# Two ordinary pairs instead of three at the head of each FFN, with the copies of turned tokens moved and the token sums reordered

## The chip, the cores and the metric

The kernel runs on one core of a Trainium2 chip. The metric is device time of one execution in microseconds (us); lower is better. Engines are named as in the profile: PE (TensorE matmul), PEld (its weight load), DVE (VectorE), ACT (ScalarE), POOL (GpSimd) and SP (SyncE, which here only issues DMAs).

## The reference

One encoder layer on 512 tokens of 1024 features, in float32: a half-step SwiGLU FFN, token mixing by two attention branches, and a second half-step SwiGLU FFN, each between two RMS norms. The change touches the two FFNs:

```python
D_MODEL, SEQ, D_FF = 1024, 512, 2816
def _rmsnorm(x, g):
    y = x * lax.rsqrt(jnp.mean(x * x, axis=-1, keepdims=True) + 1e-6)
    return y * g
def _swiglu(x, w_gate, w_up, w_down):
    return (jax.nn.silu(x @ w_gate) * (x @ w_up)) @ w_down
...
f = _swiglu(_rmsnorm(x, ffn1_pre_g[l]), ffn1_w_gate[l], ffn1_w_up[l], ffn1_w_down[l])
x = x + 0.5 * _rmsnorm(f, ffn1_post_g[l])
h = _rmsnorm(x, mix_pre_g[l])
# ... two attention branches on h, gated, projected, normed and added to x
f = _swiglu(_rmsnorm(x, ffn2_pre_g[l]), ffn2_w_gate[l], ffn2_w_up[l], ffn2_w_down[l])
x = x + 0.5 * _rmsnorm(f, ffn2_post_g[l])
```

## The kernel before

**Exactness.** Each float32 operand is split into a high part (`hi`, a cast to a shorter format, on ACT) and a low part (`lo`, what is left, a subtraction on DVE); `split` does both. A product is then three matmuls (`mm3`): high by high, high by low, low by high (lines 153 to 155).

**Tokens.** After a norm, the tokens are turned (tokens along the free axis) by PE transposes into a PSUM bank `pt`, four feature blocks at a time (`turned`, for token tile `t` of 128 and feature half `b`). From `pt`, ACT writes `hn_hi` and DVE `hn_lo`. For the last 256 tokens (`t > 1`), ACT also keeps the unsplit value in four tiles `whole[b][i]`, as long as the list `whole` is not empty.

**A pair.** `gate` and `up` of 128 hidden features make a pair `j`; an FFN has 22 (`NF`). An ordinary pair takes two pieces of weights (128x1024 each) and does 2 x 8 x 3 = 48 matmuls of 512 columns. The first two pairs are done together in `first_pairs`: four projections over tokens 0 to 255, with the turning of tokens 256 to 511 put between them, then the same four over tokens 256 to 511. `use` makes the hidden value of a pair: SiLU on ACT and a multiplication on DVE (line 436).

**Seven products.** The remaining pairs go through `seven`, a scheme of Strassen's kind over (gate, up) x (two feature halves) x (two token halves): seven products of 4 x 3 matmuls of 256 columns instead of eight, 84 in all for a pair. Its moving operands 1, 2 and 4 are plain parts of `hn`; 3, 5, 6 and 7 are sums over tokens, made and split once for each FFN by `combined` (lines 242 and 235 on DVE, 85 and 86 for the split into tiles `v`). Its stationary operands are blocks of weights and their sums: `load_blocks` loads five (four DMAs on SP's queue, and two DMAs that accumulate, on POOL's queue, lines 266 and 267), `sums_of` makes two more on DVE (lines 272, 273), and `split_block` splits each into a tile `w`. `ready(j, i)` does this for block `i` of pair `j`, one pair ahead of the products.

**Order.** The program is written in one order, and a planner lays out the queue of each engine from it with its own estimate of times: what is ready and was written earlier goes first. An engine then works through its queue in that fixed order. In some stretches (`ordered`) the written order is kept as it is on PE, ACT and DVE: from the start of the kernel, or from the last part of `token_major`, up to the end of the matmuls of `first_pairs`. `use`, `combined` and `seven` lie outside. On SP the written order is kept up to the end of the first FFN. Tiles come from pools: 54 `unit` tiles of 128x512, 12 tiles `w`, 2 tiles `raw`, and 8 PSUM banks; a tile is given back after its last use in the program.

**Streams.** `fetch` converts the next piece of weights of the ordinary stream, up to `state["stop"]`, and calls `state["ahead"]` where there is none. At the end of each FFN the products of the down projection follow in `token_major`. The mixing between the FFNs calls `first_pairs` too, with `then` making copies of all turned tokens in another order (`v_proj_na`; line 524 on ACT, 526 on DVE).

Of the kernel before, what the change touches and what calls it, by code (L numbers as in the profile page):

```python
# [12 lines left out]
F32 = mybir.dt.float32  # L13
# [18 lines left out]
SPREAD = 4  # L32
URGENT = 400
TURN = 1
STD = 3
WARM = (0, 0, 0, 5, 15)
PINNED = (mybir.EngineType.PE, mybir.EngineType.Activation, mybir.EngineType.DVE)

# [2 lines left out]
def block_kernel(ctx, tc, x, gains, weights, rpb_near, rpb_all, alibi0, alibi12, out):  # L41
# [13 lines left out]
    def unit(dt=F32, name="u"):  # L55
        return up.tile([P, 512], dt, tag="u", name=name)
# [27 lines left out]
    def split(hi, lo, src):  # L84
        nc.scalar.copy(hi, src)  # L85
        nc.vector.tensor_tensor(lo, src, hi.bitcast(F32), op=ALU.subtract)  # L86
# [56 lines left out]
    late = deque()  # L143
    next_norm = []
    whole = []

    def step(n=1):
        for _ in range(n):
# [22 lines left out]
    def first_pairs(use, turns, then=None):  # L171

        w = [take(False) for _ in range(4)]
        ps = [bank() for _ in range(4)]
        for i in range(4):
            proj_into(ps[i], w[i], 0, 256)
            if i in turns:
                late.popleft()()
                if next_norm:
                    next_norm.pop()()  # L180
        if then:
            then()
        fetch()
        fetch()
        for i in range(4):
            proj_into(ps[i], w[i], 256, 512)
        ordered[-1].append(mark())
        use(0, *ps[:2])
        use(1, *ps[2:])
# [28 lines left out]
    def turned(t, b, xs):  # L218
        pt = bank()
        for i in range(4):  # L220
            nc.tensor.transpose(pt[:, i * P:(i + 1) * P], xs[:, i * P:(i + 1) * P], ident)  # L221
        to = (slice(None), slice(4 * b, 4 * b + 4), slice(t * P, (t + 1) * P))
        pt = pt.rearrange("p (k t) -> p k t", t=P)
        nc.scalar.copy(hn_hi[to], pt)
        nc.vector.tensor_tensor(hn_lo[to], pt, hn_hi[to].bitcast(F32), op=ALU.subtract)
        if whole and t > 1:
            for i in range(2):
                o = whole[b][i].rearrange("p (k t) -> p k t", k=2)
                nc.scalar.copy(o[:, :, (t - 2) * P:(t - 1) * P], pt[:, 2 * i:2 * i + 2])

    def combined():


        sub, add = ALU.subtract, ALU.add
        tt = lambda a, b, op: (lambda u: [nc.vector.tensor_tensor(u, a, b, op=op), u][1])(unit(name="sum"))
        view = lambda a, b, i: a[:, 4 * b + 2 * i:4 * b + 2 * i + 2, 0:256]
        flat = lambda u: u.rearrange("p (k t) -> p k t", k=2)
        mv = {i: [] for i in (3, 5, 6, 7)}
        for i in range(2):
            a = [unit(name="sum"), unit(name="sum")]  # L240
            for b in range(2):
                nc.vector.tensor_tensor(flat(a[b]), view(hn_hi, b, i).bitcast(F32), view(hn_lo, b, i).bitcast(F32), op=add)
            c, d = whole[0][i], whole[1][i]
            v = {7: tt(a[0], c, sub), 5: tt(c, d, sub)}
            v[6] = tt(v[5], a[0], sub)
            v[3] = tt(v[6], a[1], add)
            for n in (5, 6, 3, 7):
                hi, lo = unit(F32R, "v"), unit(F32R, "v")
                split(hi, lo, v[n])
                mv[n] += [(hi[:, k * 256:k * 256 + 256], lo[:, k * 256:k * 256 + 256]) for k in range(2)]  # L250
        whole.clear()
        for n, b, t in ((1, 0, 0), (2, 1, 0), (4, 1, 1)):
            mv[n] = [(hn_hi[:, 4 * b + k, t * 256:t * 256 + 256], hn_lo[:, 4 * b + k, t * 256:t * 256 + 256])
                     for k in range(4)]
        return mv

    def load_blocks(n):


        r = wp.tile([P, PIECE], F32, tag="raw", name="raw", bufs=2)  # L260
        w11, t1, t3 = unit(name="w11"), unit(name="t1"), unit(name="t3")
        nc.sync.dma_start(t1, weights[n + 1][:, :512])
        nc.sync.dma_start(t3, weights[n + 1][:, :512])
        nc.sync.dma_start(r, weights[n])
        nc.sync.dma_start(w11, weights[n + 1][:, 512:])
        nc.gpsimd.dma_start(t1, weights[n][:, :512], accum_op=ALU.add)
        nc.gpsimd.dma_start(t3, weights[n + 1][:, 512:], accum_op=ALU.add)
        return {1: r[:, :512], 2: r[:, 512:], 3: w11, 5: t1, 7: t3}
# [9 lines left out]
        split(w[:, :512], w[:, 512:], raw)  # L278
        return w

    def seven(use, mv, n_pairs, n0, behind):

        raws = {}
        blocks = {}
        o = {}

        def get(j):
            if j < n_pairs:
                raws[j] = load_blocks(n0 + 2 * j)

        def ready(j, i):
            if j < n_pairs:
                if j and loads:
                    loads.popleft()()
                if i == 1:
                    sums_of(raws[j])  # L300
                blocks[j, i] = split_block(raws[j].pop(i))
            elif behind:
                behind()

        def product(j, i, key, start):
            if start:
                o[key, j] = bank(key)
            w = blocks.pop((j, i))
            acc = o[key, j][:, :256]
            for k in range(4):  # L310
                mm3(acc, w[:, k * P:(k + 1) * P], w[:, 512 + k * P:512 + (k + 1) * P], *mv[i][k],
                    start and k == 0, k == 3, skip_group_check=True)
            return acc

        res = {}
        get(0)
        get(1)
        for i in (1, 5, 2, 6, 3, 7, 4):
            ready(0, i)
        for j in range(n_pairs + 1):  # L320
            now, was = j < n_pairs, j > 0
            get(j + 2)
            if now:
                q = product(j, 1, "q", True)
                g, u = res[j] = unit(name="g"), unit(name="up")
                nc.scalar.copy(g[:, :256], q)
            ready(j + 1, 1)
            if was:
                q0 = product(j - 1, 7, "q", False)
                g0, u0 = res.pop(j - 1)  # L330
                nc.vector.tensor_tensor(u0[:, 256:], u0[:, 256:], q0, op=ALU.subtract)
            ready(j + 1, 5)
            if now:
                p = product(j, 5, "p", True)
                nc.scalar.copy(u[:, 256:], p)
            ready(j + 1, 2)
            if now:
                r = product(j, 2, "r", True)
                nc.vector.tensor_tensor(g[:, :256], g[:, :256], r, op=ALU.add)
            ready(j + 1, 6)  # L340
            if now:
                product(j, 6, "q", False)
                nc.scalar.copy(u[:, :256], q)
            ready(j + 1, 3)
            if was:
                product(j - 1, 4, "q", False)
                use(j - 1, g0, u0, q0)
            ready(j + 1, 7)
            if now:
                product(j, 3, "p", False)  # L350
                nc.vector.tensor_tensor(u[:, :256], p, u[:, :256], op=ALU.subtract)
            ready(j + 1, 4)
# [68 lines left out]
    def ffn(g, store, src):  # L421
        hidden = [None] * NF
        parts = {}
        n0 = state["take"]

        def stat(k):
            if k not in parts:
                parts[k] = unit(F32R), unit(F32R)
                split(*parts[k], hidden[k])
                hidden[k] = None  # L430
            return parts[k]

        def use(j, pg, pu):
            h = unit(name="h")
            nc.scalar.activation(h, pg, AF.Silu)
            nc.vector.tensor_tensor(h, pu, h, op=ALU.mult)
            hidden[j] = h

        def use7(j, g, u, q):
            nc.scalar.activation(g[:, :256], g[:, :256], AF.Silu)  # L440
            nc.scalar.activation(g[:, 256:], q, AF.Silu)
            nc.vector.tensor_tensor(g, u, g, op=ALU.mult)
            hidden[STD + j] = g

        first_pairs(use, (0, 2) if store else (1, 2))
        mv = combined()
        g_post, g_pre = gain(g), None if store else gain(g + 1)
        for j in range(2, STD):
            pair(use, j)
        if not store:  # L450
            bias_plan()
        after = n0 + 2 * NF
        state["stop"] = total if store else total - 3 * NF + 2 * STD

        def behind():
            state["next"] = max(state["next"], after)
            state["take"] = after
            fetch()

        seven(use7, mv, NF - STD, n0 + 2 * STD, behind)  # L460
        token_major(NF, stat, g_post, 4.0, g_pre, store, src)


# [647 lines left out]
```

## Time and profile before

| | |
|---|---|
| time, median of 3 runs | 1131.28 us (1131.22 to 1131.42) |
| the profiled execution | 1130.41 us |
| its span, first to last instruction | 1128.6 us |
| mean granted TensorE clock | 0.996 |
| PE busy | 1113.6 us (99%) |
| DVE busy | 720.1 us (64%) |
| ACT busy | 582.6 us (52%) |
| POOL busy | 99.7 us (9%) |
| DMA, mean over the span | 138 GB/s |

A row of the timeline gives start, duration, engine, line, operation, what is written and read, shapes and the count of like instructions in a row; in brackets stands how long the engine was idle before, and what ended that. Matmuls are pipelined: a row of 0.28 us may be followed by the next start after 0.12 us, so PE's rate is read from starts. A row of the waits gives total us, how often, and the longest. A row of the windows gives a stretch, then for each engine its busy us and its count of instructions, the granted clock, the share of the DMA engines and GB/s.

### The profile page before, as it was taken

The page shows a single profiled execution, that of the slowest core. Times are in us where ns is not written, and L with a number is a line of the kernel's source. Part 1 is how long each engine was busy: PE and PEld are TensorE (multiplying, and loading weights), DVE is VectorE, ACT ScalarE, POOL GpSimd, SP SyncE. Part 2 cuts the span into 40 slices and gives each one's busy share as a digit, 9 for nine tenths or more (in the row PEclk, how much of TensorE's full clock was granted, in tenths as well). Part 3 has the DMA queues.
Part 4 walks back from the last instruction along what each step waited for, and adds up shares of the span by engine and source line. Part 5 has one row for each costly group of instructions (what it writes and reads, how often), then busy time and mean ns, then how long its engine had stood idle before and what let it go on. Part 6 is the DMA issues. An engine that isn't in the chain of part 4 may idle for free.

```text
span 1128.6 us, 18242 instructions
## 1 busy us (share of the span) xinstructions
PE 1113.6 (99%) x6956; PEld 1005.7 (89%) x6956; DVE 720.1 (64%) x1327; ACT 582.6 (52%) x1188; POOL 99.7 (9%) x157
## 2 busy tenths in 40 slices
PE   8999999999999999999999999999999999999997
PEld 6899999998888988888988888889899999998886
DVE  5797777773245677877486635655787777782312
ACT  5465555572233676767646632345555555571210
POOL 3111221000002000000000000013111111100001
PEclk8999999999999999999999999999999999999999
DMA  6789988443353353322223223353687677443511
GB/s 217 193 191 242 247 222 194 118 126 113 99 156 124 103 169 115 124 89 76 76 81 90 79 79 100 89 181 109 154 215 173 169 192 187 122 132 97 170 51 74
DMA packets 77430, 156.23 MB, mean 138 GB/s; under 512 B 22048, under 2 KB 24096, under 8 KB 77344
## 3 DMA queue, kind: packets, MB, share of 16 engines
q1 hardware_dynamic: 64000, 134.96, 37.7%
q0 software_dynamic: 10944, 19.93, 11.2%
q8 instruction: 54, 0.88, 0.3%
q10 hardware_dynamic: 2400, 0.20, 0.1%
q14 instruction: 32, 0.26, 0.1%
HBM read 150.02 MB, written 7.58 MB: 140 GB/s over the span
## 4 chain that ended last, share of the span: by engine, by line
PE 94%; DVE 2%; ACT 1%; DMA 1%; issue 0%; SPq 0%; DVEq 0%; POOLq 0%; POOL 0%; ACTq 0%
PE ps L153 18%; PE ps L154 18%; PE ps L155 18%; PE q L155 6%; PE q L154 6%; PE q L153 6%; PE p L155 3%; PE p L153 3%; PE p L154 3%; PE r L155 2%; PE r L153 2%; PE r L154 2%; PE ps L661 1%; PE ps L221 1%; PE ps L688 1%; PE ps L630 1%
## 5 line engine op out<-in xcount | busy, mean ns | idle before, releaser
L86 DVE TENSOR_TENSOR w<-raw,w 128x1024 fp32r<-128x1024 f32 (+1 forms) x200 | 195.0, 979 | 217.7 <-ACT w L85 211.4
L85 ACT CAST w<-raw 128x1024 fp32r<-128x1024 f32 (+1 forms) x200 | 169.6, 853 | 239.9 <-PE ps L154 162.8
L153 PE MATMUL ps<-hn_hi,w 128*128 128x512 f32 (+1 forms) x512 | 181.3, 355 | 0.0
L154 PE MATMUL ps<-hn_lo,w 128*128 128x512 f32 (+1 forms) x512 | 179.5, 351 | 0.0
L155 PE MATMUL ps<-hn_hi,w 128*128 128x512 f32 (+1 forms) x512 | 179.2, 350 | 0.0
L153 PE MATMUL ps<-w,u 128*128 128x512 f32 (+1 forms) x456 | 177.3, 389 | 0.0
L154 PE MATMUL ps<-w,u 128*128 128x512 f32 (+1 forms) x456 | 176.9, 388 | 0.0
L155 PE MATMUL ps<-w,u 128*128 128x512 f32 (+1 forms) x456 | 176.8, 388 | 0.0
L86 DVE TENSOR_TENSOR w<-t,w 128x512 fp32r<-128x512 f32 x152 | 104.3, 689 | 28.1 <-ACT w L85 28.1
L85 ACT CAST w<-t 128x512 fp32r<-128x512 f32 x152 | 93.7, 619 | 43.1 <-DVE t L272 18.4
L155 PEld LDWEIGHTS ps<-hn_hi,w 128*128 128x128 f32 x512 | 97.0, 189 | 12.8
L154 PEld LDWEIGHTS ps<-hn_lo,w 128*128 128x128 f32 x512 | 97.2, 190 | 11.6
L153 PEld LDWEIGHTS ps<-hn_hi,w 128*128 128x128 f32 x512 | 97.1, 190 | 11.8 <-issue 0.3
L155 PEld LDWEIGHTS ps<-w,u 128*128 128x128 f32 x456 | 85.7, 188 | 17.5
L154 PEld LDWEIGHTS ps<-w,u 128*128 128x128 f32 x456 | 85.7, 188 | 17.0
L153 PEld LDWEIGHTS ps<-w,u 128*128 128x128 f32 x456 | 85.7, 188 | 16.9
L155 PE MATMUL q<-hn_hi,w 128*128 128x256 f32 x304 | 86.4, 284 | 1.8 <-DVE w L86 1.8
L155 PE MATMUL p<-v,w 128*128 128x256 f32 x304 | 85.9, 284 | 0.9 <-DVE w L86 0.9
L154 PE MATMUL q<-v,w 128*128 128x256 f32 x304 | 86.2, 283 | 0.0
L153 PE MATMUL p<-v,w 128*128 128x256 f32 x304 | 86.2, 283 | 0.0
L155 PE MATMUL q<-v,w 128*128 128x256 f32 x304 | 86.2, 283 | 0.0
L154 PE MATMUL q<-hn_lo,w 128*128 128x256 f32 x304 | 86.2, 283 | 0.0
(149 smaller groups left out, 2299.8 us busy)
## 6 DMA issues: line engine op xcount, KB each, us to landing
raw<-in_weights_dram SPq DMA_DIRECT2D x156, 512.0 KB
t<-in_weights_dram SPq DMA_DIRECT2D x76, 256.0 KB
t<-in_weights_dram POOLq DMA_DIRECT2D x76, 256.0 KB, 5.5
w<-in_weights_dram SPq DMA_DIRECT2D x38, 256.0 KB
x<-in_x_dram SPq DMA_DIRECT2D x16, 256.0 KB
gain<-in_gains_dram SPq DMA_DIRECT2D x6, 512.0 KB
table<-bias_d SPq DMA_DIRECT2D x12, 256.0 KB
table<-in_alibi_dram SPq DMA_DIRECT2D x8, 256.0 KB
```

The source lines that it names most:

```text
L85: nc.scalar.copy(hi, src)
L86: nc.vector.tensor_tensor(lo, src, hi.bitcast(F32), op=ALU.subtract)
L153: nc.tensor.matmul(o, sh, mh, start=start, stop=False, **kw)
L154: nc.tensor.matmul(o, sh, ml, start=False, stop=False, **kw)
L155: nc.tensor.matmul(o, sl, mh, start=False, stop=stop, **kw)
L221: nc.tensor.transpose(pt[:, i * P:(i + 1) * P], xs[:, i * P:(i + 1) * P], ident)
L630: nc.tensor.matmul(ps[:, o:o + w], q[:, cols], windows(wide, kl, i), start=False, stop=True)
L661: nc.tensor.transpose(ps[:, i * P:(i + 1) * P], s, ident)
L688: nc.tensor.matmul(o, vv[n][:, h], m, start=first, stop=(n == 3 and part == 1), skip_group_check=True)
```

## The change

`STD`, the number of ordinary pairs, goes from 3 to 2, so each FFN has 20 pairs in `seven` where it had 19. The copies into `whole` are no longer issued in `turned`; they are collected in `kept` and issued by `first_pairs` after its first four half projections. `load_blocks` for the first two pairs of `seven` is called from the two `fetch` calls in `first_pairs`, by way of `state["ahead"]`. `combined` becomes a generator: first four sums of `hn_hi` and `hn_lo`, then, at each `next`, the sums and splits of operand 5, 6, 3 and 7 in turn, called from the loop that readies the first blocks, whose order becomes 1, 2, 5, 6, 3, 7, 4. `whole.clear()` now stands behind the last `yield`.

```diff
-STD = 3
+STD = 2
...
+    kept = deque()
...
     def first_pairs(use, turns, then=None):
...
+        while kept:
+            kept.popleft()()
         if then:
             then()
         fetch()
...
         if whole and t > 1:
-            for i in range(2):
-                o = whole[b][i].rearrange("p (k t) -> p k t", k=2)
-                nc.scalar.copy(o[:, :, (t - 2) * P:(t - 1) * P], pt[:, 2 * i:2 * i + 2])
+            kept.append(lambda: keep(t, b, pt))
+
+    def keep(t, b, pt):
+        for i in range(2):
+            o = whole[b][i].rearrange("p (k t) -> p k t", k=2)
+            nc.scalar.copy(o[:, :, (t - 2) * P:(t - 1) * P], pt[:, 2 * i:2 * i + 2])
...
     def combined():
...
-        whole.clear()
+        mv = {}
         for n, b, t in ((1, 0, 0), (2, 1, 0), (4, 1, 1)):
             mv[n] = [(hn_hi[:, 4 * b + k, t * 256:t * 256 + 256], hn_lo[:, 4 * b + k, t * 256:t * 256 + 256])
                      for k in range(4)]
-        return mv
+        a = [[unit(name="sum"), unit(name="sum")] for _ in range(2)]
+        for b in range(2):
+            for i in range(2):
+                nc.vector.tensor_tensor(flat(a[b][i]), view(hn_hi, b, i).bitcast(F32), view(hn_lo, b, i).bitcast(F32), op=add)
+        yield mv
+        v = {}
+        for n, of in ((5, lambda i: (whole[0][i], whole[1][i], sub)), (6, lambda i: (v[5][i], a[0][i], sub)),
+                      (3, lambda i: (v[6][i], a[1][i], add)), (7, lambda i: (a[0][i], whole[0][i], sub))):
+            v[n] = [tt(*of(i)) for i in range(2)]
+            mv[n] = []
+            for i in range(2):
+                hi, lo = unit(F32R, "v"), unit(F32R, "v")
+                split(hi, lo, v[n][i])
+                mv[n] += [(hi[:, k * 256:k * 256 + 256], lo[:, k * 256:k * 256 + 256]) for k in range(2)]
+            yield mv
+        whole.clear()
...
-    def seven(use, mv, n_pairs, n0, behind):
+    def seven(use, sums, n_pairs, n0, behind, raws):
...
-            if j < n_pairs:
+            if j < n_pairs and j not in raws:
                 raws[j] = load_blocks(n0 + 2 * j)
...
-        for i in (1, 5, 2, 6, 3, 7, 4):
+        for i in (1, 2, 5, 6, 3, 7, 4):
             ready(0, i)
+            if i not in (1, 2, 4):
+                mv = next(sums)
...
+        raws = {}
+
+        def soon():
+            if len(raws) < 2:
+                raws[len(raws)] = load_blocks(n0 + 2 * STD + 2 * len(raws))
+
+        state["ahead"] = soon
         first_pairs(use, (0, 2) if store else (1, 2))
-        mv = combined()
+        state["ahead"] = lambda: None
+        sums = combined()
+        next(sums)
...
-        seven(use7, mv, NF - STD, n0 + 2 * STD, behind)
+        seven(use7, sums, NF - STD, n0 + 2 * STD, behind, raws)
```

More of the change, by code (lines that the diff above doesn't have):

```diff
@@ L237, in combined @@
         flat = lambda u: u.rearrange("p (k t) -> p k t", k=2)
[L238 to L250, printed above, removed]
-        whole.clear()
+        mv = {}
         for n, b, t in ((1, 0, 0), (2, 1, 0), (4, 1, 1)):
@@ L279, in split_block @@
         return w
-    def seven(use, mv, n_pairs, n0, behind):
-        raws = {}
+    def seven(use, sums, n_pairs, n0, behind, raws):
         blocks = {}
```

## The prediction

> **What bounds the kernel now.** I read the page first, then PE's waits, then PE's pace by windows, and last the timeline of DVE around the two FFN heads.
>
> ```profile
> span 1128.6 us, 18242 instructions
> PE 1113.6 (99%) x6956; PEld 1005.7 (89%) x6956; DVE 720.1 (64%) x1327; ACT 582.6 (52%) x1188; POOL 99.7 (9%) x157
> ...
> PE ps L221 <- DVE u L960: 3.1, 1, 3.1
> PE q L155 <- DVE w L86: 1.8, 2, 1.2
> PE p L155 <- DVE w L86: 0.9, 1, 0.9
> PE ps L629 <- DVE u L86: 0.8, 1, 0.8
> ```
>
> PE is busy from end to end. Of its waits, the first is the start of the kernel; the next two rows, 2.7 us in three places, are the heads of the two FFNs, where products wait for the low parts of weight blocks. A matmul row of 0.28 us outlasts its slot of 0.12, which hides 0.16 us at each place, so the heads cost 2.7 + 3 x 0.16 = 3.2 us. Everything else must come from PE's work itself, or from new waits.
>
> ```profile
> core 0: us, PE busy (x) PEld busy (x) DVE busy (x) ACT busy (x) POOL busy (x), PEclk, DMA share, GB/s
> 40.71:51.62 10.91, 10.91 (x51) 9.02 (x49) 9.91 (x16) 5.43 (x10) 3.52 (x4) 1.00 0.97 238
> 51.62:61.70 10.08, 8.86 (x73) 8.66 (x72) 9.81 (x17) 7.77 (x18) 0.00 (x0) 1.00 0.36 88
> 100.00:110.08 10.08, 10.08 (x86) 10.08 (x85) 8.35 (x16) 6.62 (x16) 1.77 (x2) 1.00 0.99 235
> 808.40:818.10 9.70, 8.17 (x66) 7.77 (x65) 9.70 (x17) 8.76 (x19) 0.67 (x1) 1.00 0.42 135
> ```
>
> The first window is the third ordinary pair of the first FFN: 48 matmuls (three more overlap its edges) in 10.91 us, 0.227 us each. The third is a pair of seven products in full flow: 84 (two more at the edges) in 10.08 us, 0.120 each, without a wait. The second and fourth are the first seven products of each FFN: DVE busy 9.81 of 10.08 and 9.70 of 9.70, PE idle. At a head DVE is the bound.
>
> **The pair exchanged.** Each FFN gives up 10.91 us of PE and takes 10.08: 2 x 0.83 = 1.66 us less. The ACT and DVE work of the twentieth seven-pair, and its larger loads, lie in a stage where DVE is busy 8.35 of 10.08 and PE does not wait: nothing. The pieces no longer converted free ACT and DVE before the head, which is counted below.
>
> **The head without its cover.** How DVE's queue runs at the second FFN's head, and the first's:
>
> ```profile
> 785.33 0.69 DVE L225 TENSOR_TENSOR hn_lo<-ps,hn_hi 128x512 fp32r<-128x512 f32 x1 [1.20 <-ACT hn_hi L224]
> 793.77 0.69 DVE L436 TENSOR_TENSOR h<-ps,h 128x512 f32<-128x512 f32 x1 [7.75 <-PE ps L155]
> 794.38 1.28 DVE L242 TENSOR_TENSOR sum<-hn_hi,hn_lo 128x512 f32<-128x512 f32 x2
> 795.58 0.69 DVE L235 TENSOR_TENSOR sum<-sum,whole 128x512 f32<-128x512 f32 x1
> 796.18 0.69 DVE L235 TENSOR_TENSOR sum<-whole 128x512 f32<-128x512 f32 x1
> 796.90 0.69 DVE L235 TENSOR_TENSOR sum<-sum 128x512 f32<-128x512 f32 x1
> 799.53 0.69 DVE L436 TENSOR_TENSOR h<-ps,h 128x512 f32<-128x512 f32 x1 [1.94 <-PE ps L155]
> 800.14 0.68 DVE L235 TENSOR_TENSOR sum<-sum 128x512 f32<-128x512 f32 x1
> ...
> 33.83 1.23 DVE L86 TENSOR_TENSOR w<-raw,w 128x1024 fp32r<-128x1024 f32 x1 [0.35 <-ACT w L85]
> 35.15 0.69 DVE L436 TENSOR_TENSOR h<-ps,h 128x512 f32<-128x512 f32 x1
> 35.76 1.28 DVE L242 TENSOR_TENSOR sum<-hn_hi,hn_lo 128x512 f32<-128x512 f32 x2
> 40.98 0.69 DVE L436 TENSOR_TENSOR h<-ps,h 128x512 f32<-128x512 f32 x1 [2.01 <-PE ps L155]
> 51.89 0.69 DVE L436 TENSOR_TENSOR h<-ps,h 128x512 f32<-128x512 f32 x1 [0.93 <-PE ps L155]
> ...
> 817.84 0.42 DVE L339 TENSOR_TENSOR g<-g,r 128x256 f32<-128x256 f32 x1
> 818.17 0.69 DVE L86 TENSOR_TENSOR w<-t,w 128x512 fp32r<-128x512 f32 x1
> ```
>
> Three readings. A 128x512 instruction takes 0.60 us from start to start (794.38 to 795.58 for two), a small one 0.33 (817.84 to 818.17). The token sums (L242) read only tokens that were turned long before, yet at both heads none runs before the first pair's multiplication (L436), even with DVE idle 7.75 us. And DVE waits in line: at 799.53 it sat 1.94 us before a multiplication while the sum behind it had its inputs at 797.6.
>
> Now the tally. Before PE can start the second seven-pair, DVE does in the changed head: 2 multiplications, 4 sums L242, 8 sums L235, 8 low parts of `v`, 2 sums of blocks, 7 low parts of blocks, and 3 for the next pair (two sums, one low part): 34 x 0.60 = 20.4, and two small additions, 0.7: 21.1 us. The method holds before: 35 such instructions from 35.06 (with a third multiplication), 21.0 + 0.7, and waits of 2.01 + 0.93 give 59.7; five products from 51.62 on need 5 x 12 x 0.120 = 7.2, to 58.8. It gives 0.9 us of wait where the window shows 1.2.
>
> ```profile
> 782.82 0.59 ACT L224 CAST hn_hi<-ps 128x512 fp32r<-128x512 f32 x1 [1.76 <-PE ps L221]
> 376.28 1.08 ACT L224 CAST hn_hi<-ps 128x512 fp32r<-128x512 f32 x2 [4.58 <-PE ps L221]
> 376.90 1.29 DVE L225 TENSOR_TENSOR hn_lo<-ps,hn_hi 128x512 fp32r<-128x512 f32 x2 [3.04 <-ACT hn_hi L224]
> 25.27 1.03 PE L221 MATMUL ps<-ident,u 128*128 128x128 f32 x8
> ...
> 781.77 0.33 SPq L262 DMA_DIRECT2D t<-in_weights_dram  x1
> 787.14 0.94 POOL L266 DMA_DIRECT2D t<-in_weights_dram  x1 [8.76 <-DMA t<-in_weights_dram]
> ```
>
> Second FFN: with the `whole` copies gone from between, both low parts of the last tokens end 1.9 us after the first cast (376.28 to 378.2), at 782.82 + 1.9 = 784.7, where DVE is free. Block loads start no later than now (781.77) and their accumulation is issued by 788, so the low parts of blocks 1, 2 and 5 (1.8 us) can come early. The first multiplication comes at 791.9: 793.77, less eight of the third pair's matmuls that now stand among the second halves (8 x 0.23 = 1.9). DVE waits 7.2 - 1.8 = 5.4 us. Then that multiplication, the four L242 and one more (five stood there before) take 3.6, to 795.5; the second multiplication cannot start before 799.53 - 1.9 = 797.7: 2.2 more. DVE is done at 784.7 + 21.1 + 5.4 + 2.2 = 813.4. PE ends the second halves at 797.4 and has seven products (1, 2, 5, 6, 3, 7 and 4) for 10.1 us, to 807.5. It waits 5.9 us. First FFN: four of the last eight transposes are done at 25.8 (half of 25.27 to 26.3), and 1.9 later, at 27.7, DVE is free; the multiplications come at 35.0 and 41.0, the second halves end at 40.7. The same sum gives 27.7 + 21.1 + 5.5 + 2.4 = 56.7 against 50.8, 5.9 again. Together 11.8 against 3.2 now: 8.6 us more. From both sides: none of these waits on DVE, and PE waits 0; no early blocks and product 4 only behind the second pair's first, 5.9 + 1.8 + 1.4 = 9.1 a head. I take 5.9, from how both heads ran.
>
> **Copies.** In the FFNs eight copies (2.6 us of ACT) move behind the casts; their readers, the sums for operand 5, come after 791.9, so this costs nothing unless the sums start early. But `whole` is no longer emptied: the generator is left at its last `yield`. So the mixing between the FFNs now makes eight copies it did not make:
>
> ```profile
> 30.63 0.65 ACT L229 COPY whole<-ps 128x256 f32<-128x256 f32 x2 [0.76 <-DVE hn_lo L225]
> 377.24 9.16 ACT L524 CAST u<-hn_hi 128x128 fp32r<-128x128 f32 x16
> 386.31 1.04 ACT L85 CAST w<-raw 128x1024 fp32r<-128x1024 f32 x1
> 387.38 1.23 DVE L86 TENSOR_TENSOR w<-raw,w 128x1024 fp32r<-128x1024 f32 x1 [4.23 <-ACT w L85]
> 391.35 0.40 PE L155 MATMUL ps<-w,u 128*128 128x512 f32 x1
> 398.50 0.36 PE L629 MATMUL ps<-u 128*128 128x256 f32 x1 [0.80 <-DVE u L86]
> ```
>
> Four times 0.65 is 2.6 us, in front of the 16 copies that `then` makes. The weights' low part, which PE needs at 391.35, is done at 388.6: 2.7 us of slack, just used up. The scores at 398.50 already wait 0.80; their chain hangs on the same ACT queue. Between 0 (the planner puts other matmuls ahead) and 2.6 (the whole delay on PE) I take 0.5, nearer to 0 as more such matmuls are at hand. Four units held longer: nothing.
>
> **Loads moved.** Each `soon` issues four DMAs on SP and two on POOL, ahead of the gains' loads on SP. The gains are read hundreds of us later: nothing. In the first FFN POOL's two issues may stand ahead of the norm of the last tokens; I take 0 for it, with an upper bound of 2 us, the two issues at about 1 us each.
>
> **Sum.** -1.7 + 8.6 + 0.5 = +7.4 us. The profiled execution took 1130.41 (span 1128.6 and 1.8 around it), 0.9 under the median of 1131.28; on the median: 1138.7 us.
>
> **The rivals.** *DVE does not wait* (faster): the planner brings the four L242, the sums for operand 5 and the early blocks ahead of the first multiplication. Then 784.7 + 21.1 = 805.8 is before 807.5, and PE waits nowhere: -1.7 - 3.2 + 0.5 = -4.4, 1126.9 us. For it: data and blocks are there sooner than before, and at both heads DVE has time. Against: neither head shows one sum ahead of its multiplication. It decides where DVE's waits at a head, 7.6 us, fall under about 3.9: then PE waits 2.2 a head and the gain pays for it. *Half of it*: one head fills the wait, the other not, or both partly: about 1131, no change that can be told; a measurement of this kernel tells 0.2%, 2.3 us. *The clock falls*: PE's waits come in one piece and the granted clock drops, as after the 3.1 us at the start:
>
> ```profile
> 12.00:16.00 4.00, 4.00 (x16) 2.75 (x15) 3.24 (x5) 3.88 (x8) 2.43 (x2) 0.50 0.88 341
> ```
>
> Four us at 0.50 lose 2 us, for two heads 4: 1142.7. The waits here come between products, at most 2 us each, and the windows with PE idle 1.2 and 1.5 us kept 1.00. The Trainium skill (TensorE: Matmul & The Clock Gate, Part 1: The HAM clock gate) says that the clock halves after an idle window of about 3.4 us; by that rule my waits keep it, and one long wait would not. The trace agrees at its start.
>
> **How the numbers follow.** Slower as worked out 0.57, with the fall of the clock 0.06; half of it 0.17; DVE does not wait 0.20. The likeliest alone is 1133.8 (second waits filled, -4.4, mixing 0) to 1144. The whole range, 1126.5 to 1144, reaches to the faster rival, since the cases have both signs. Faster 0.20, same 0.15, slower 0.65.
>
> **What would show it.** Right: DVE idle before the first and second L436 of each head, L242 behind it, PE's waits on DVE at `p` and `q` several times today's 2.7 us, spread over the first seven-pair; 84 matmuls each 10.08 us after it; eight L229 at 377 us. Wrong: L242 and L235 before the first L436 and no waits of PE.

## The result, and the profile after

The changed kernel takes 1142.37 us (median; 1141.74 to 1146.02), the kernel before 1131.25 beside it: a ratio of 1.0105, 95% interval 1.0084 to 1.0127. It is 11.1 us slower. The profile is of the execution that took 1146.02.

The head of the page:

```profile
span 1144.2 us, 18459 instructions
PE 1118.0 (98%) x7028; PEld 1012.5 (88%) x7028; DVE 730.1 (64%) x1347; ACT 591.7 (52%) x1214; POOL 102.9 (9%) x161
```

PE has 72 matmuls more than the 6956 of before (two seven-pairs of 84 for two ordinary pairs of 48) and 4.4 us more of busy time, and the span is 15.6 us longer: PE waits. Of the 15.6 us, 11.3 lie in the two FFNs (worked out below), 3.05 in the mixing between them and about 1 at the start. Its waits (total us, times, longest):

```profile
PE p L154 <- ACT v L85: 5.5, 2, 2.7
PE q L154 <- ACT g L335: 4.7, 2, 2.4
PE ps L224 <- DVE u L978: 4.7, 1, 4.7
PE ps L679 <- DVE u L667: 1.9, 2, 1.7
```

The first two rows are new: at each head PE waits once for the cast of operand 5 (`v`) and once for ACT's copy of product 1 out of bank `q`, which product 6 is to fill further. Two shorter waits, 0.7 and 0.3 us, follow at the second head. Before, the heads showed only 2.7 us, for low parts of blocks. The last two rows are the start and a place in the mixing; both are longer in this execution (3.1 us before at the start).

The first two seven-pairs of each FFN by windows: before (the first two rows), after (the next two), then a stretch of the first changed head. Behind the busy times stands the granted clock.

```profile
51.62:73.24 21.62, 20.40 (x169) 20.20 (x168) 21.35 (x38) 14.96 (x33) 1.73 (x2) 1.00 0.60 134
808.36:830.55 22.19, 20.66 (x170) 20.26 (x168) 21.23 (x38) 15.66 (x34) 3.94 (x5) 1.00 0.74 204
```

```profile
41.11:69.83 28.72, 23.72 (x170) 23.32 (x169) 27.91 (x48) 17.77 (x37) 3.41 (x4) 0.88 0.63 139
807.16:835.82 28.66, 22.48 (x170) 21.66 (x169) 28.08 (x49) 17.57 (x36) 5.21 (x6) 0.94 0.73 183
46.00:50.00 4.00, 4.00 (x23) 4.00 (x22) 4.00 (x8) 0.07 (x1) 0.00 (x0) 0.57 0.57 147
```

168 matmuls at 0.120 us are 20.16. Before, these stretches lost 1.5 and 2.0 us; now they lose 8.6 and 8.5, with DVE busy nearly throughout. In 46 to 50, PE starts 23 matmuls where 0.120 us would allow 33.

DVE at the first head, then at the second:

```profile
35.62 0.69 DVE L445 TENSOR_TENSOR h<-ps,h 128x512 f32<-128x512 f32 x1 [4.01 <-PE ps L156]
...
36.83 2.49 DVE L251 TENSOR_TENSOR sum<-hn_hi,hn_lo 128x512 f32<-128x512 f32 x4
...
41.38 0.69 DVE L445 TENSOR_TENSOR h<-ps,h 128x512 f32<-128x512 f32 x1 [1.46 <-PE ps L156]
...
42.59 1.29 DVE L241 TENSOR_TENSOR sum<-whole 128x512 f32<-128x512 f32 x2
43.79 0.69 DVE L86 TENSOR_TENSOR w<-t,w 128x512 fp32r<-128x512 f32 x1
...
48.01 1.29 DVE L86 TENSOR_TENSOR v<-sum,v 128x512 fp32r<-128x512 f32 x2
...
799.86 0.69 DVE L86 TENSOR_TENSOR w<-t,w 128x512 fp32r<-128x512 f32 x1 [5.41 <-ACT w L85]
801.60 0.69 DVE L445 TENSOR_TENSOR h<-ps,h 128x512 f32<-128x512 f32 x1 [1.05 <-PE ps L156]
802.21 2.49 DVE L251 TENSOR_TENSOR sum<-hn_hi,hn_lo 128x512 f32<-128x512 f32 x4
...
807.43 0.69 DVE L445 TENSOR_TENSOR h<-ps,h 128x512 f32<-128x512 f32 x1 [2.13 <-PE ps L156]
```

This is the order that was forecast. The token sums (line 242 before, 251 now) run only behind the first multiplication (436 before, 445 now), with DVE idle 4.0 us and 6.5 us (5.41 and 1.05) ahead of it, and the sums for operand 5 only behind the second. The low parts of the blocks then stand ahead of those of operand 5. Then PE, at each wait of the two heads, and ACT's last casts of `v`:

```profile
42.43 0.28 PE L156 MATMUL q<-hn_hi,w 128*128 128x256 f32 x1
45.45 0.39 PE L154 MATMUL p<-v,w 128*128 128x256 f32 x1 [2.75 <-ACT v L85]
...
54.12 0.28 PE L156 MATMUL r<-hn_hi,w 128*128 128x256 f32 x1
56.65 0.58 PE L154 MATMUL q<-v,w 128*128 128x256 f32 x1 [2.25 <-ACT g L335]
57.02 0.42 PE L155 MATMUL q<-v,w 128*128 128x256 f32 x1
57.24 0.41 PE L156 MATMUL q<-v,w 128*128 128x256 f32 x1
...
819.97 0.28 PE L156 MATMUL r<-hn_hi,w 128*128 128x256 f32 x1
822.69 0.38 PE L154 MATMUL q<-v,w 128*128 128x256 f32 x1 [2.45 <-ACT g L335]
822.92 0.28 PE L155 MATMUL q<-v,w 128*128 128x256 f32 x1
```

```profile
55.10 1.22 ACT L85 CAST v<-sum 128x512 fp32r<-128x512 f32 x2 [1.36 <-DVE sum L241]
56.23 0.37 ACT L335 COPY g<-q 128x256 f32<-128x256 f32 x1
```

Less its slot of 0.12 us, the first wait cost 2.90 us at each head, the second 2.41 and 2.60 (a start at 56.65 instead of 54.24). The copy that ended the second stands in ACT's queue behind the casts of all operands, and these wait for DVE's sums. By PE's starts over the 168 matmuls, the longer waits add up to 5.3 and 6.8 us, and slow matmuls (0.213 instead of 0.120 us, 57.02 to 57.24 for one) to 3.1 and 1.7.

The whole of an FFN by PE's starts, from its first projection to its last product: before 236.80 and 236.62 us, after 242.51 and 242.25. The two differences, 5.71 and 5.63, make 11.3: all of the change lies there. The kernel with the kept list emptied (in the table below) has the same heads and 242.49 and 242.25 us in an execution of 1140.84 us, so these stretches are not peculiar to the slower execution that was profiled here.

### The profile page after: what moved, and what is told of

It reads as the page before. It is cut to its first block, busy times and chain, and to the rows that moved or that the text cites. A ratio compares the mean times of both kernels' runs of the same rounds, so it can differ in the third digit from the quotient of the medians.

```text
span 1144.2 us, 18459 instructions
## 1 busy us (share of the span) xinstructions
PE 1118.0 (98%) x7028; PEld 1012.5 (88%) x7028; DVE 730.1 (64%) x1347; ACT 591.7 (52%) x1214; POOL 102.9 (9%) x161
## 4 chain that ended last, share of the span: by engine, by line
PE 92%; DVE 3%; ACT 3%; DMA 1%; issue 1%; SPq 0%; DVEq 0%; POOLq 0%; POOL 0%; ACTq 0%
PE ps L154 18%; PE ps L155 18%; PE ps L156 18%; PE q L154 7%; PE q L156 7%; PE q L155 7%; PE p L154 3%; PE p L155 3%; PE p L156 3%; PE r L155 2%; PE r L154 2%; PE r L156 2%; PE ps L679 1%; PE ps L224 1%; PE ps L706 1%; DVE w L86 1%
## 5 line engine op out<-in xcount | busy, mean ns | idle before, releaser
L154 PE MATMUL ps<-hn_hi,w 128*128 128x512 f32 (+1 forms) x480 | 169.4, 353 | 0.0
L155 PE MATMUL ps<-hn_lo,w 128*128 128x512 f32 (+1 forms) x480 | 167.4, 349 | 0.0
L156 PE MATMUL ps<-hn_hi,w 128*128 128x512 f32 (+1 forms) x480 | 167.1, 348 | 0.0
L86 DVE TENSOR_TENSOR w<-t,w 128x512 fp32r<-128x512 f32 x160 | 109.7, 688 | 34.5 <-ACT w L85 34.0
L85 ACT CAST w<-t 128x512 fp32r<-128x512 f32 x160 | 99.0, 620 | 40.3 <-ACT w L85 18.9
L156 PEld LDWEIGHTS ps<-hn_hi,w 128*128 128x128 f32 x480 | 91.2, 190 | 11.7
L154 PEld LDWEIGHTS ps<-hn_hi,w 128*128 128x128 f32 x480 | 91.3, 190 | 10.6
L155 PEld LDWEIGHTS ps<-hn_lo,w 128*128 128x128 f32 x480 | 91.4, 190 | 10.4
L154 PE MATMUL p<-v,w 128*128 128x256 f32 x320 | 91.3, 286 | 5.8 <-ACT v L85 5.5
L154 PE MATMUL q<-v,w 128*128 128x256 f32 x320 | 91.4, 286 | 4.7 <-ACT g L335 4.7
L154 PE MATMUL q<-hn_hi,w 128*128 128x256 f32 x320 | 90.9, 285 | 0.7 <-ACT w L85 0.7
L155 PE MATMUL q<-v,w 128*128 128x256 f32 x320 | 91.1, 285 | 0.0
L156 PE MATMUL q<-v,w 128*128 128x256 f32 x320 | 91.1, 285 | 0.0
L155 PE MATMUL q<-hn_lo,w 128*128 128x256 f32 x320 | 90.9, 284 | 0.0
```

The lines of the kernel that those rows point to most:

```text
L154: nc.tensor.matmul(o, sh, mh, start=start, stop=False, **kw)
L155: nc.tensor.matmul(o, sh, ml, start=False, stop=False, **kw)
L156: nc.tensor.matmul(o, sl, mh, start=False, stop=stop, **kw)
```

## The experiments

Two numbers say how each kernel's FFNs went: the same stretch in FFN 1 and 2, from its profile, in us. The ratio is to the kernel before as it was measured beside each (medians 1131.10 to 1131.25).

| kernel | us | ratio, 95% interval | FFN 1 | FFN 2 |
|---|---|---|---|---|
| before | 1131.25 | 1 | 236.80 | 236.62 |
| changed | 1142.37 | 1.0105 (1.0084, 1.0127) | 242.51 | 242.25 |
| three pairs, new order | 1139.16 | 1.0072 (1.0057, 1.0087) | 245.12 | 236.97 |
| two pairs, old order | 1150.86 | 1.0181 (1.0164, 1.0198) | 247.43 | 246.31 |
| kept list emptied | 1141.23 | 1.0092 (1.0077, 1.0107) | 242.49 | 242.25 |
| operands 5 and 6 early | 1135.45 | 1.0043 (1.0028, 1.0058) | 239.81 | 238.35 |
| product 2 before 5 | 1142.56 | 1.0097 (1.0084, 1.0111) | 242.48 | 243.08 |
| first wait filled | 1142.67 | 1.0099 (1.0086, 1.0113) | 242.82 | 242.94 |
| all sums early, two pairs | 1128.43 | 0.9977 (0.9968, 0.9986) | 236.29 | 235.98 |
| all sums early, three pairs | 1128.52 | 0.9974 (0.9965, 0.9984) | 236.89 | 234.59 |
| and emptied, two pairs | 1128.90 | 0.9981 (0.9972, 0.9989) | 236.02 | 235.98 |
| and blocks first, two pairs | 1129.10 | 0.9983 (0.9974, 0.9992) | 235.78 | 235.61 |
| and blocks first, three pairs | 1129.30 | 0.9983 (0.9974, 0.9992) | 237.56 | 234.59 |

**The parts of the change alone.** `-STD = 2` `+STD = 3` in the changed kernel:

> The changed kernel with three ordinary pairs again; everything else of the change stays. My theory: the cover over DVE's queue is what was lost. In the two stretches of the first two seven-pairs the changed kernel spent 28.7 us (41.11 to 69.83, and 807.16 to 835.82) on 168 matmuls that take 20.2 at 0.120 us; the kernel before spent 21.6 and 22.2. With 10.9 us of ordinary matmuls between the first pairs and the products again, DVE's queue is ahead and the heads lose 1 to 2 us each as before: 1128 to 1133 us, 9 to 14 under the changed kernel's 1142.4. Rival, the new order of sums and copies itself costs (block casts ahead of operand 5's cast on ACT, the copies in the mixing): the 10.9 us of cover then hide only part and the time stays above 1135.

`-STD = 3` `+STD = 2` in the kernel before:

> The kernel before with two ordinary pairs and nothing else of the change. My theory: the same DVE tally at each head with the same multiplications in front of it, and the sums of all operands in one block; the heads lose at least what they lose in the changed kernel (8.5 us each), so 1142 to 1150 us. If the new order of sums and blocks is what costs, this kernel is clearly faster than the changed one, 1131 to 1138 us.

The first expectation was wrong and its rival held: the time stayed above 1135. The second was right in its theory, and 0.9 us above its range. Two pairs alone cost 19.7 us, and the new order then saves 8.5; with three pairs the new order costs 8.0. The two-pair kernel in the old order puts all operands ahead of the blocks, and PE waits for the first blocks in one piece at each head:

```profile
PE q L153 <- ACT w L85: 9.4, 1, 9.4
PE p L153 <- ACT w L85: 9.2, 1, 9.2
```

With three pairs in the new order, DVE at the first head:

```profile
34.68 2.49 DVE L251 TENSOR_TENSOR sum<-hn_hi,hn_lo 128x512 f32<-128x512 f32 x4
...
46.36 0.69 DVE L86 TENSOR_TENSOR w<-raw,w 128x512 fp32r<-128x512 f32 x1 [5.84 <-ACT w L85]
50.66 0.69 DVE L445 TENSOR_TENSOR h<-ps,h 128x512 f32<-128x512 f32 x1 [3.61 <-PE ps L156]
...
53.68 1.29 DVE L241 TENSOR_TENSOR sum<-whole 128x512 f32<-128x512 f32 x2
```

The stretch from 31 us to the end of its third pair, and the same window of the kernel before:

```profile
31.00:50.50 19.50, 19.50 (x122) 17.61 (x121) 5.03 (x8) 3.34 (x6) 5.45 (x6) 1.00 0.90 222
```

```profile
31.00:50.50 19.50, 19.50 (x127) 17.80 (x126) 15.69 (x24) 8.70 (x16) 5.51 (x6) 1.00 0.84 219
```

DVE worked 5.0 us in this stretch where it had worked 15.7. The generator puts the sums of operands 5, 6, 3 and 7 behind the third pair in the written order, and here they run behind its multiplication at 50.66. So cover alone is not the cause, as I had it: DVE must also have the work ahead of the multiplications. In the second FFN the same kernel lost only 0.35 us against before, and there DVE's queue had another order:

```profile
807.80 1.29 DVE L241 TENSOR_TENSOR sum<-whole 128x512 f32<-128x512 f32 x2
...
817.23 0.68 DVE L445 TENSOR_TENSOR h<-ps,h 128x512 f32<-128x512 f32 x1
```

Between the second multiplication, at 805.87, and the third, at 817.23, stood 12 instructions, among them operand 5's sums and the low parts of blocks; in the first FFN a single one stood there. That agrees with the reading.

**The copies in the mixing.** `+next(sums, None)` behind the loop that readies the first blocks, so that the kept list is emptied:

> The changed kernel with one more step of the generator after the first blocks, so that the list of kept tokens is emptied and the mixing makes no eight copies. The prediction's step: 0.5 us faster (bounds 0 and 2.6). From the traces since: the first scores of the mixing came 6.67 us late in the changed kernel, exactly as late as the first projections of the mixing, so the eight copies (2.3 us on ACT) cost nothing: within 0.5 us of the changed kernel, 1142. If the 3.05 us that the profiled execution lost between the first score and the second FFN come from the copies: 1139 us.

It was 1.1 us faster than the changed kernel, more than the 0.5 expected, but with intervals that overlap (1.0077 to 1.0107 against 1.0084 to 1.0127). With all sums early the emptied list gave 1128.90 against 1128.43, again with intervals that overlap:

> All sums early and two pairs, and besides the list of kept tokens emptied behind the last sum, so that the mixing makes no eight copies. The prediction's step: 0.5 us less than all sums early (bounds 0 and 2.6), so 1127.9. From the traces since, in which the mixing was as long with the copies as without, up to its first scores: 0, 1128.4 us.

In the changed kernel the copies are there, ahead of the 16 of `then`:

```profile
383.90 2.33 ACT L235 COPY whole<-ps 128x256 f32<-128x256 f32 x8
386.02 9.16 ACT L542 CAST u<-hn_hi 128x128 fp32r<-128x128 f32 x16
```

From the first projection of the mixing to its first score PE took 30.21 us before and 30.22 after: the copies cost nothing there. The 3.05 us that the changed kernel's profile lost later in the mixing are absent from the other kernels with the copies (from the mixing's first projection to the second FFN's 409.59 us in the changed kernel, 406.06 with all sums early, 407.37 with the first wait filled, the longest of them, and 406.54 before).

**DVE's order itself.** The sums are drawn from the generator inside `first_pairs`, in the stretch whose written order is kept:

```diff
...
-        first_pairs(use, (0, 2) if store else (1, 2))
+        sums = combined()
+        first_pairs(use, (0, 2) if store else (1, 2), lambda: [next(sums) for _ in range(3)])
         state["ahead"] = lambda: None
-        sums = combined()
-        next(sums)
```

> The changed kernel with the four token sums and the sums and splits of operands 5 and 6 issued inside the first pairs, behind the first four half projections (in the stretch whose written order is kept), so that DVE does them in the 4 to 5 us in which it stood idle ahead of the first multiplication: 12 instructions of 0.60 us, 7.2 us. My theory (DVE in line behind the multiplications is what PE waits for): PE's waits of 5.5 us on operand 5's cast and 4.7 on the copy of product 1 in the profile of the changed kernel go almost wholly, the clock keeps, and 11 to 15 us come back: 1127 to 1132 us. Rival (the order in the queues of PE and ACT: the block casts ahead of operand 5's cast, the copy of product 1 behind the casts of all operands): operand 5's wait goes since its cast is early, but the copy is still behind the casts of 3 and 7 and the blocks, so that about half stays: 1135 to 1138 us.

The 1135.45 us lie in the rival's range, but the profile does not bear the rival out: the wait for the copy was 0.7 us in all. What was left were 3.9 us of waits for low parts of blocks, 1.6 for casts of blocks and some 16 slow matmuls at the first head, with DVE idle where there was room for more:

```profile
34.25 0.68 DVE L445 TENSOR_TENSOR h<-ps,h 128x512 f32<-128x512 f32 x1
39.75 0.69 DVE L445 TENSOR_TENSOR h<-ps,h 128x512 f32<-128x512 f32 x1 [4.82 <-PE ps L156]
```

So all five steps of the generator were drawn there, `range(5)`:

> The changed kernel with all twenty-odd token instructions early: the four token sums and the sums and splits of operands 5, 6, 3 and 7 (20 DVE instructions, 12 us) are issued inside the first pairs, behind the first four half projections; the list of kept tokens stays as in the changed kernel. In the run with operands 5 and 6 early DVE had done 12 of them by 34.3 us and then stood idle 4.82 us before the second multiplication at 39.75; eight more take 4.8 us. My theory (DVE's order is the bound): after 40.4 only seven low parts and two sums of blocks are left, 9 x 0.60 = 5.4 us for products of 10.1 us; a head loses about 1.5 us, the wait for the first block's low part, instead of 8.5: 1127 to 1131 us, 11 to 15 under the changed kernel. Rival (the pair exchange itself costs, or ACT's order of casts): no better than operands 5 and 6 early, 1134 to 1136 us.

```profile
26.26 2.48 DVE L251 TENSOR_TENSOR sum<-hn_hi,hn_lo 128x512 f32<-128x512 f32 x4
...
37.79 1.29 DVE L86 TENSOR_TENSOR v<-sum,v 128x512 fp32r<-128x512 f32 x2
39.00 1.28 DVE L446 TENSOR_TENSOR h<-ps,h 128x512 f32<-128x512 f32 x2
```

Its first two seven-pairs, by windows:

```profile
39.90:60.93 21.03, 20.50 (x168) 20.29 (x169) 19.30 (x34) 14.62 (x32) 3.14 (x4) 1.00 0.74 154
795.24:817.62 22.38, 20.86 (x171) 20.34 (x170) 21.13 (x39) 16.53 (x36) 3.43 (x4) 1.00 0.73 189
```

DVE goes from the last tokens at 26.3 us through all operands to the multiplications without a stop, the heads lose 0.9 us (and 0.91 just ahead of the window, where the first product waited for its cast) and 2.2, and the clock stays at 1.00. The work is the same as in the changed kernel; only its place differs, and 13.9 us went with it. Against the kernel before it is 2.7 us faster, 0.2%. Of that the FFNs show 1.15 us; in the two profiles 1.2 us more lie at the start (first projection at 13.99 instead of 15.20), and no run ties those to the change. With three pairs:

> The same with three ordinary pairs. My theory for the three-pair run that stayed at 1139.2 us: the generator put the sums of operands 5, 6, 3 and 7 behind the third pair's multiplication in DVE's queue (they ran from 53.7 us on, behind the multiplication at 50.66, with DVE idle 2.5, 2.7, 5.8 and 3.6 us before); with the sums early that loss goes: 1126 to 1130 us. With both heads free of waits the difference between this run and the one with two pairs is the pair exchange alone, 1.66 us in favour of two pairs, less what a head with two pairs still loses. Rival (the three-pair run's loss came from the copies or the loads moved): it stays above 1135.

This too came out as my theory had it, and it removes the whole loss of the first experiment.

**PE's and ACT's queues.** Product 2 of the first seven-pair is written ahead of product 5:

> The changed kernel with product 2 of the first seven-pair written ahead of product 5, so that PE does not stand before operand 5's cast with a product ready behind it. Theory DVE-bound: the second wait of a head ends with ACT's copy at 56.5 and 822.6 us whatever PE did before, so the time won at the first wait is lost at the second: 0 to 1 us, 1141 to 1143. Rival (PE's own order costs): 1.44 us a head and the clock that does not fall, 1136 to 1139 us.

The first wait falls to 1.47 us (and 0.66 for a low part), the second grows to 4.55; in PE's waits:

```profile
PE q L154 <- ACT g L335: 8.8, 2, 4.4
```

ACT's copy, in the timeline, comes when operand 7 is cast, here at 55.2 (56.2 in the changed kernel, whose start was 1.0 us later):

```profile
55.22 0.37 ACT L335 COPY g<-q 128x256 f32<-128x256 f32 x1
```

**The clock.** The first wait is filled with matmuls whose result is overwritten:

```diff
...
+                if j == 0:
+                    fill_in(2)   # product 1's 12 matmuls twice, into bank p
                 p = product(j, 5, "p", True)
```

> The changed kernel with the 12 matmuls of product 1 of the first seven-pair repeated twice, into the bank of product 5 (which starts it anew), between product 1 and product 5: 24 x 0.12 = 2.9 us of matmuls where PE waited 2.9 us at the first wait of each head; the rest as it is. If the fall of the clock after that wait (15 matmuls at 0.213 instead of 0.120 us) costs time: 1.4 us a head, 1139 to 1140 us. If it only eats into the second wait, whose end ACT's copy sets: within 1 us of the changed kernel, with the granted clock at 1.00 after the first wait and a second wait longer by about 1.4 us.

PE's wait, a window behind the place of the first wait, and ACT's copy:

```profile
PE q L154 <- ACT g L345: 7.7, 2, 3.9
```

```profile
46.00:50.00 4.00, 4.00 (x36) 4.00 (x35) 4.00 (x7) 0.45 (x1) 0.00 (x0) 1.00 0.45 90
```

```profile
55.84 0.36 ACT L345 COPY g<-q 128x256 f32<-128x256 f32 x1
```

The clock held at the place of the first wait (36 matmuls in 4 us, where the changed kernel started 23), and nothing was won: the second wait grew from 2.41 and 2.60 to 4.00 and 4.01 us, since ACT's copy ended it no earlier (40.4 us behind the first projection, 40.1 in the changed kernel). Both runs say that DVE, by way of ACT's copy, sets the head, not the order in PE's queue and not the first fall of the clock. A kernel with this copy ahead of the casts was not run. Behind the second wait a fall has nothing to hide in: here slow matmuls cost 1.7 and 2.3 us there.

**What is left.** With all sums early and the list emptied, the multiplications of the first two pairs (with the SiLU on ACT that each needs) are put behind the splits of blocks 1 and 2:

```diff
         for i in (1, 2, 5, 6, 3, 7, 4):
             ready(0, i)
+            while pend and i == 2:
+                pend.pop(0)()      # use() of the first two pairs
...
```

> As the run before it, and the multiplications of the first two pairs are written behind the splits of blocks 1 and 2, so that DVE makes the low parts of the first blocks before them. With all sums early the heads still lost 0.9 us (a product's third matmul waited 0.69 for block 1's low part at 40.8, and the product 0.91 for its cast) and 2.2 us in the second FFN. My theory (what is left of the head is DVE's and ACT's order too): 1.5 to 3 us less, 1125.5 to 1127 us. Rival (the blocks come late from memory, or the multiplications' place holds back PSUM): no gain, 1128 to 1129.

> The same with three ordinary pairs. With no waits at the heads in either kernel, the difference to the run with two pairs is the pair exchange by itself: the prediction's term is 2 x 0.83 = 1.66 us, so 1.7 us slower than with two pairs, about 1128 us. If the exchange is worth nothing, the two are equal.

Both expectations were missed: 1129.10 and 1129.30, no gain, and no difference by the pair exchange. With two pairs the heads still lost about 1.9 us each; in the first, the waits for block 1 shrank from 0.91 and 0.69 us to 0.47, and one of 1.08 came six us later. So the waits moved and hardly shrank. The scores of the mixing waited 1.4 us for a low part, 0.4 more than with all sums early and the list emptied.

## Why the prediction was right, and where it was off

**The mechanism was right.** DVE idle ahead of the multiplications, with the token sums behind them, and PE's waits spread over the first seven-pair were forecast and seen (the rows name ACT, whose casts wait for DVE's sums); doing the same sums early removed them. The faster rival failed at the point that it named: at neither head did a sum come ahead of the first multiplication.

**The size of the heads was too small.** The waits were forecast as 5.9 us a head; they were 5.3 and 6.8. But the slow matmuls take part of the first wait's time out of the second, so the two are counted together. From the first matmul of `seven` to the first of product 6 (41.11 to 56.65, and 807.16 to 822.69) PE took 15.5 us at each head. It started 72 matmuls in that time, products 1, 5 and 2 of two pairs, which take 8.64 us at 0.120: 6.9 us lost, 1.0 over the forecast. In the filled kernel, without the first fall, the waits were 2.88 (the 24 matmuls) and 4.0: 6.9 again. The step that failed was the place where PE stops. The end of DVE's work was forecast well: operand 7's low parts were done 40.8 and 40.6 us behind the first projection, where the sum has 41.5 and 40.7. But the sum lets PE run seven products, 10.1 us, before it waits for that end. Product 6 already needs ACT's copy, and this stood behind the casts of operands 3 and 7, so PE had only six products to run: 1.44 us less, of which 0.3 came back because the copy ended the wait that much before DVE was through.

**The clock was held wrongly at 1.00.** The step that said "at most 2 us each" failed: a head's wait came in two pieces of 2.4 to 2.9 us, and the clock fell at three of the four. That left 4.5 us out of the likeliest case, 1138.7. The rival with the fall, at 1142.7 us and a chance of 0.06, is what came, nearly to the number. It had one long wait at each head in mind, though, and not two shorter ones, so that part of the closeness is luck. By the terms measured: waits 5.3 + 6.8 instead of 3.2 before, +8.9; slow matmuls 3.1 + 1.7 against 0.3 before, +4.5; the exchange, -1.7; together +11.7, where 11.1 was measured.

**The exchange was sized rightly.** In the second FFN the three-pair kernel with all sums early loses nothing at its head and takes 234.59 us; with two pairs it takes 235.98, of which the head loses 2.22: 233.76, or 0.83 less, the forecast term. But it bought no time in any kernel run here: 1128.43 against 1128.52, and 1129.10 against 1129.30. In the second FFN the shorter cover cost its head more than the exchange gave (235.98 against 234.59, and 235.61 against 234.59); in the first, two pairs were shorter (236.29 against 236.89, and 235.78 against 237.56).

**The copies cost nothing that shows** where 0.5 was taken; that is the lower bound of the step. The loads moved were taken at 0 with a bound of 2 us in the first FFN. That FFN grew by 5.71 us and the second, without that bound, by 5.63; no run moves the loads alone.

What stays open: why the planner ordered the two heads of the three-pair kernel differently, and what the head would take with ACT's copy ahead of the casts.

## What to carry to other kernels

On an engine with a fixed queue, count not only how much work must be done by a time, but what each piece stands behind. Work whose inputs are early belongs ahead of an instruction that waits for PE: here 20 sums and splits moved there turned +11.1 us into -2.7. Before a cover is shortened, move what it covers, and expect nothing of the shorter cover until the waits behind it are gone; and when a wait in the middle is removed, look at which instruction ends the next one.

## What the runs showed of the hardware

The granted clock fell after waits of 2.90 us at both heads (start to start, less a slot), after 2.41 us at the first, and after 4.0 in the filled kernel, but not after 2.60 at the second head, where matmuls went on at 0.12 (822.92 to the next). With operands 5 and 6 early it fell even behind a wait of 1.66 us:

```profile
46.54 0.28 PE L155 MATMUL q<-hn_lo,w 128*128 128x256 f32 x1
48.32 0.58 PE L156 MATMUL q<-hn_hi,w 128*128 128x256 f32 x1 [1.50 <-DVE w L86]
48.69 0.42 PE L154 MATMUL q<-hn_hi,w 128*128 128x256 f32 x1
```

There another wait stood shortly before it: from 45.14 to 48.32, 3.2 us, PE had started only two matmuls. The length of a single wait did not decide.

The fall did not always begin at once: after the first wait at 45.45 matmuls ran at 0.12 for another 0.9 us and then some 16 at 0.213, 3.4 us. Other slow stretches lasted 2.9 us (811.51 to 814.45) and, in the filled kernel, 5.1 (820.07 to 825.14). The Trainium skill (TensorE: Matmul & The Clock Gate, Part 1: The HAM clock gate) says that the monitor's window of about 3.4 us runs freely and that one idle window lowers the clock. The 3.4 us of slow matmuls agree with such a window, and a free phase would fit the varying delay; no run here shows the phase. That an idle window is needed does not agree: PE's waits here were shorter than 3.4 us and still lowered the clock, and so did the wait of 3.1 us at the start that the prediction took as agreeing. So the rule as used in the prediction was no safe bound.
